# Three moves around the scan and the norms of an RWKV-7 layer: late row splits, steps of 5, block products ten matmuls later

## The chip, the cores and the metric

The kernel runs on one core of a Trainium2 chip. The metric is the device time of one execution in microseconds, as the median of several runs. Besides the runs there is one profiled execution, whose trace gives every instruction of the engines: TensorE (PE, with its weight loads as PEld), VectorE (DVE), ScalarE (ACT), GpSimd (POOL) and SyncE (SP), which issues most DMAs. Each engine goes through its own instructions in the order in which they were put.

## The reference, cut to what matters

Two residual layers on x of 512 tokens by 2048 channels, all in float32: layer 0 is gated differential attention, layer 1 is gated RWKV-7 time mixing with 32 heads of 64 channels. The change lies in layer 1:

```python
p = h @ w_in                                   # r, k, v, g, and two narrow projections
p = p + (token_shift(p) - p) * mu
...
kk = kk / max(norm(kk), 1e-12); k = k * (1 + (a - 1) * k_a)
y = wkv7_scan(r, decay, k, v, -kk, kk * a)     # S = S*w + (S a) b^T + v k^T ; y = S r, token by token
y = (y - mean(y)) * rsqrt(var(y) + GN_EPS) * gn_w + gn_b      # per head: the "norm" below
y = y + sum(r * k * r_k) * v
y = y * silu(g)
x = x + y @ w_out                              # the out-projection
```

## The kernel before, in words

Channels lie on the 128 partitions, tokens along the free axis, so that a tile of 128 x 512 holds one pair of heads for all tokens. Every large product is done as three matmuls of 128x512 on operands split in two parts (`mm3`, L124): hi x hi, hi x lo, lo x hi. Weights come in as `wraw`, ACT casts the hi part `wh` (L105), DVE makes the lo part `wl` (L106). In the same way a row of 128 channels of y that goes into the out-projection is split into `hH` (ACT, L452) and `hL` (DVE, L453), a "row split".

Layer 1 goes through 16 rounds, j = 0 to 15, one for each pair of heads. In a round PE does the projections of pair j (and of the next pair's keys and receptances), and between their matmuls the scan of pair j-1. The scan is in chunks: 512 tokens are 8 chunks, and within a chunk the recurrence is solved as a triangular system.

- `gram` (L1345 pt, L1362 gp) makes the products of a pair inside its chunks out of `AR` (L1335) and `BK`. `t_solve` (L1410 to L1430, 31 short pairs of DVE steps L1421 and L1423) solves a triangular half; its result goes through DRAM (`td`, written in L1431, loaded as `TT` in L1450).
- `t_combine` joins the halves: DVE transposes T out of TT (L1460, two instructions, one per head), PE makes the block products px (L1466), ACT copies X (L1469), PE makes the second block products (L1477) and ACT copies them into TT (L1480).
- `scan_pair` has 8 steps. In each PE makes sm out of the state VS and G (L1559), ACT copies it as rhs (L1562), PE multiplies rhs with TT (L1570), ACT copies VS (L1572), PE makes the product with BKT (L1577), and DVE makes the next VS (L1581, the first time L1584). So every step goes three times from PE to another engine and back. Then come the outputs Y (L1599, L1603) and the subtraction of the mean (L1614 to L1616).
- `group_norm` makes the rest of the norm: squares (ACT, L1625), their sum (L1627), a dozen small steps for the reciprocal root (L1628, L64 to L71) and yc times rsg (L1631). `finish_y` transposes yc on PE (L1638) and adds it into y (L1640). `gated` multiplies with the gate (L1532) and writes the row of y into DRAM (`yd`, POOL, L1533).
- `gate` makes the gate's tile mixv out of its projection: ACT L1188, DVE L1189, ACT's tanh L1521, DVE L1525.

What sets the order of the scan among the projections is the `Chain`: the steps of `chain(...)` are a generator that yields the number of large matmuls to pass before the next step; `tick` counts them. `delay` is the first of these numbers, `lead` stands ahead of the two transpositions L1460, `GAP_T` = 8 ahead of px, `GAP_X` = 10 ahead of L1477, `gap` and `gap_s` are the distances between the products of the scan. `lead` has a default of 10 and an entry of its own in `leads` for some rounds (LAG is 2). A scheduler then orders the instructions of each engine by priority and by what each needs; `issue_after(ins)` makes it place an instruction behind another.

After round 15 the last pair's chain runs among the gate projections of pairs 14 and 15 and the first part of the out-projection. The out-projection takes 16 rows of y: rows 0 to 13 are loaded from `yd` by SP (L462) into eight tiles (the later six rows use the tiles of the first six again) and split; rows 14 and 15 are split from mixv and mixE in place. The gate tile mixv is one buffer: L1188 of pair 14 overwrites the one out of which row 13 is written to DRAM.

## Time and profile before

| | |
|---|---|
| median of the runs | 2062.27 us (2060.34 to 2063.82) |
| the profiled execution's own time | 2061.87 us |
| its span | 2060.2 us |
| PE busy | 2041.7 us, 99% |
| DVE busy | 1608.8 us, 78% |
| ACT busy | 1135.5 us, 55% |
| POOL busy | 385.2 us, 19% |
| TensorE clock granted | 1.0 over the span |

Line numbers are those of the kernel above. In a timeline row stand the start in us from the span's start, the duration in us, the engine, the line, the operation with out<-in, the shapes, how many instructions the row joins, and in brackets the idle time of the engine ahead of it with what ended it. In the chain that ended last a row has start, duration, engine, tile and line. A row of the waits names the waiting instruction, the one waited for, and total, times and longest in us.

### The profile page before, as it was taken

What the parts mean: (1) busy time and instruction counts of PE and PEld (TensorE: products, weight loads), DVE (VectorE), ACT (ScalarE), POOL (GpSimd) and SP (SyncE); (2) the same over time, 40 slices, a digit from 0 to 9 for tenths busy, and PEclk for the clock granted to TensorE, in tenths of its full rate; (3) what the DMA queues carried; (4) which work ended last, traced back from release to release, by engine and by line L of the source; (5) the groups of instructions that cost most, each with busy time, mean ns of one, the idle gap of its engine ahead of it and who ended that gap; (6) DMA issues with size and microseconds to landing.
All of it is one profiled execution on the core that took longest, in us unless ns stands there. A gap on an engine that the chain in (4) does not pass through costs nothing.

```text
span 2060.2 us, 34171 instructions
## 1 busy us (share of the span) xinstructions
PE 2041.7 (99%) x11922; PEld 1675.0 (81%) x11922; DVE 1608.8 (78%) x4104; ACT 1135.5 (55%) x2262; POOL 385.2 (19%) x774
## 2 busy tenths in 40 slices
PE   9999999999999999999999999999999999999999
PEld 7888888888888888888877788888888888877887
DVE  7988988888888977575787888877777888767745
ACT  5765656565666544365565555555555555545423
POOL 1020111102011000101122322322222222231011
PEclk9999999999999999999999999999999999999999
DMA  8487978879787965733323323233333232346676
GB/s 285 157 163 192 178 173 184 164 193 163 190 178 170 267 218 175 171 95 107 103 77 93 92 82 96 87 96 98 98 98 98 86 96 82 111 127 200 212 180 144
DMA packets 159533, 297.76 MB, mean 145 GB/s; under 512 B 64528, under 2 KB 81936, under 8 KB 159360
## 3 DMA queue, kind: packets, MB, share of 16 engines
q1 hardware_dynamic: 110768, 184.39, 28.7%
q0 software_dynamic: 25952, 90.88, 23.3%
q10 hardware_dynamic: 22640, 20.30, 3.1%
q8 instruction: 94, 1.54, 0.3%
q14 instruction: 79, 0.65, 0.1%
HBM read 271.33 MB, written 24.18 MB: 143 GB/s over the span
## 4 chain that ended last, share of the span: by engine, by line
PE 88%; DVE 7%; ACT 3%; issue 1%; DMA 1%; ACTq 0%; SPq 0%; DVEq 0%
PE pp L124 45%; PE pp L575 23%; PE pt L124 5%; DVE wl L106 2%; PE gp L1362 2%; PE sc L124 1%; PE sm L1559 1%; PE o L124 1%; PE sm L1577 1%; PE sm L1570 1%; ACT wh L105 1%; PE Y L1599 1%; PE lora L1104 1%; PE pt L297 1%; PE z L124 1%
## 5 line engine op out<-in xcount | busy, mean ns | idle before, releaser
L106 DVE TENSOR_TENSOR wl<-wraw,wh 128x1024 fp32r<-128x1024 f32 (+1 forms) x286 | 349.9, 1223 | 165.8 <-ACT wh L105 159.1
L105 ACT CAST wh<-wraw 128x1024 fp32r<-128x1024 f32 (+1 forms) x286 | 299.4, 1047 | 237.3 <-PE pp L124 122.1
L124 PE MATMUL pp<-hL,wh 128*128 128x512 f32 x1024 | 413.8, 404 | 0.0
L124 PE MATMUL pp<-hH,wh 128*128 128x512 f32 x1024 | 412.9, 403 | 0.4 <-ACT wh L105 0.4
L124 PE MATMUL pp<-hH,wl 128*128 128x512 f32 x1024 | 413.1, 403 | 0.0
L124 PEld LDWEIGHTS pp<-hH,wh 128*128 128x128 f32 x1024 | 193.1, 189 | 34.8 <-ACT wh L105 0.6
L124 PEld LDWEIGHTS pp<-hL,wh 128*128 128x128 f32 x1024 | 193.1, 189 | 33.5
L124 PEld LDWEIGHTS pp<-hH,wl 128*128 128x128 f32 x1024 | 193.3, 189 | 32.6
L575 PE MATMUL pp<-wh,hH 128*128 128x512 f32 x448 | 176.8, 395 | 0.0
L575 PE MATMUL pp<-wh,hL 128*128 128x512 f32 x448 | 175.7, 392 | 0.0
L124 PE MATMUL pp<-wl,hH 128*128 128x512 f32 x376 | 147.5, 392 | 0.0
L124 PE MATMUL pp<-wh,hH 128*128 128x512 f32 x376 | 147.0, 392 | 0.3 <-ACT hH L1148 0.3
L124 PE MATMUL pp<-wh,hL 128*128 128x512 f32 x376 | 147.2, 392 | 0.1
L1421 DVE SCALAR_TENSOR_TENSOR tmpl<-LT,Tm 128x60 f32<-128x60 f32 (+24 forms) x496 | 135.0, 272 | 13.2
L575 PE MATMUL pp<-wl,hH 128*128 128x512 f32 x448 | 140.3, 392 | 0.0
L1565 POOL COPY SA<-VS 64x64 f32<-64x64 f32 x224 | 55.1, 246 | 398.5 <-DVE VS L1581 376.4
L1423 DVE TENSOR_TENSOR Tm<-Tm,tmpl 128x60 f32<-128x60 f32 (+24 forms) x496 | 103.6, 209 | 11.7
L1562 ACT COPY rhs<-sm 64x64 f32<-64x64 f32 x256 | 52.8, 206 | 85.6 <-PE sm L1559 82.9
L575 PEld LDWEIGHTS pp<-wl,hH 128*128 128x128 f32 x448 | 84.4, 188 | 17.2
L575 PEld LDWEIGHTS pp<-wh,hH 128*128 128x128 f32 x448 | 84.2, 188 | 17.3 <-issue 0.3
L575 PEld LDWEIGHTS pp<-wh,hL 128*128 128x128 f32 x448 | 84.2, 188 | 16.2
L1572 ACT COPY VS<-sm 64x64 f32<-64x64 f32 x256 | 52.7, 206 | 77.2 <-PE sm L1570 71.1
(432 smaller groups left out, 4375.0 us busy)
## 6 DMA issues: line engine op xcount, KB each, us to landing
wraw<-in_rw_w_in_dram SPq DMA_DIRECT2D x128, 512.0 KB
wraw<-in_da_w_in_dram SPq DMA_DIRECT2D x75, 512.0 KB
wraw<-in_da_w_in_dram POOLq DMA_DIRECT2D x28, 512.0 KB, 6.4
wraw<-in_da_w_out_dram SPq DMA_DIRECT2D x26, 512.0 KB
wraw<-in_rw_w_out_dram SPq DMA_DIRECT2D x24, 512.0 KB
Ta<-in_da_w_in_dram POOLq DMA_DIRECT2D x21, 512.0 KB, 5.6
Tb<-in_da_w_in_dram POOLq DMA_DIRECT2D x21, 512.0 KB, 5.8
Tc<-in_da_w_in_dram POOLq DMA_DIRECT2D x21, 512.0 KB, 5.5
```

The lines of the kernel that those rows point to most:

```text
L105: a = nc.scalar.copy(hi[:, ks], raw[:, ks])
L106: d = nc.vector.tensor_sub(lo[:, ks], raw[:, ks], hi[:, ks].bitcast(F32))
L124: m = nc.tensor.matmul(out, a, b, start=s, stop=e, skip_group_check=skip)
L297: nc.tensor.transpose(pt[:, c * P : (c + 1) * P], t1s[t][:, c * P : (c + 1) * P], g.ident[:])
L575: m = nc.tensor.matmul(out[t][:], x, wt[lo][:, k, :], start=first, stop=end and lo == 1 and k == KG - 1, skip_group_check=True)
L1104: m = nc.tensor.matmul(pts[i][:, s], wt[:, c : c + P], x[k][:, s], start=k == 0 and s.start == 0 and c < 2 * P and x is g.hH, stop=k == KT ...
L1362: m = nc.tensor.matmul(gp[h][:, i * P : (i + 1) * P], BK[r_, c0 + i, :, :], p.AR[r_, c0 + i, :, :], start=True, stop=True)
L1421: nc.vector.scalar_tensor_tensor(tt, LT[:, i : i + 1, i + 1 :].to_broadcast([P, s, n]), n2[:, i : i + 1], Tm[:, 0:s, i : i + 1].to_broadca ...
L1423: nc.vector.tensor_add(Tm[:, 0:s, i + 1 :], Tm[:, 0:s, i + 1 :], tt)
L1562: nc.scalar.copy(rhs[r_, :], sm[r_, h * C : h * C + C])
L1565: nc.gpsimd.tensor_copy(p.SA[r_, c - 1, :], VS[r_, c, h, :])
L1572: g.copied = nc.scalar.copy(VS[r_, c, h, :], sm[r_, P : P + C])
```

## The change

It has three parts. `group_norm` returns its last instruction (L1631), and the splits of rows 2 and later are placed behind the one of pair 14's norm. In round 15 the scan of pair 14 has five large matmuls between its products instead of four, and the last pair's chain starts after 10 instead of 24 matmuls. In round 5 (LAG + 3) the lead of pair 4's block products is 16 instead of 10.

```diff
@@ group_norm
-    nc.vector.tensor_mul(yc[:], yc[:], rs[:, :, None].to_broadcast([P, NG, C]))
+    return nc.vector.tensor_mul(yc[:], yc[:], rs[:, :, None].to_broadcast([P, NG, C])).ins
@@ layer1
-                gaps = ((6, 8) if j > LAG + 1 else (5, 6)) if full else (4, 4) if j > LAG else (4, 5)
-                leads = {1: 72, LAG: 18, LAG + 1: 42}
+                gaps = ((6, 8) if j > LAG + 1 else (5, 6)) if full else (5, 5) if j > LAG else (4, 5)
+                leads = {1: 72, LAG: 18, LAG + 1: 42, LAG + 3: 16}
@@
-        chain(g, j, p, 24, 4, 5, lead=34)
+        chain(g, j, p, 10, 4, 5, lead=34)
@@
-        group_norm(g, j - 1, pairs[j - 1])
+        normed = group_norm(g, j - 1, pairs[j - 1])
@@
-        rows = split_rows(g, g.yd2, ("r", "k", "th0", "th1", "l", "f", "xH", "xL"), 1, j - 1)
+        rows = split_rows(g, g.yd2, ("r", "k", "th0", "th1", "l", "f", "xH", "xL"), 1, j - 1, 2, (normed,))
```

On PE in round 5 the first block products px of pair 4 (L1466) move behind the gram of pair 5 (pt and gp); the rows with a minus are before, those with a plus after:

```order
 L124 MATMUL pp<-hL,wh 128x512
 L124 MATMUL pp<-hH,wl 128x512
-L1466 MATMUL px<-T_12733,G_12087 32x32 x16
 L1345 MATMUL pt<-k_12624,ones 32x128 x4
 L1362 MATMUL gp<-AR,BK 128x128 x16
+L1466 MATMUL px<-T_12733,G_12087 32x32 x16
```

The second block products L1477 came directly behind gp and now come ten matmuls behind px; the scan of pair 4 follows ten matmuls later.

On DVE in round 6, behind the subtraction of pair 4's mean (L1616), where T is transposed for pair 5 (L1460), before:

```order
L1616 TENSOR_TENSOR yc<-Y,s_13391 128x4x64 x2
L1460 STREAM_TRANSPOSE T_13420<-TT_9502 64x256 x2
L1627 TENSOR_REDUCE var<-ysq 128x8
L1628 TENSOR_SCALAR var<-var 128x8
L64 TENSOR_SCALAR rs_i<-var 128x8
```

and after:

```order
L1616 TENSOR_TENSOR yc<-Y,s_13401 128x4x64 x2
L1460 STREAM_TRANSPOSE T_13420<-TT_9502 64x256
L106 TENSOR_TENSOR wl<-wraw,wh 128x1024
L1189 SCALAR_TENSOR_TENSOR mixr<-pp,mu,mixr 128x511
L1460 STREAM_TRANSPOSE T_13420<-TT_9502 64x256
L1335 TENSOR_TENSOR AR<-mixr,E 128x8x64
```

The two transpositions stood together; now a weight's lo part and the mix of the receptances (mixr) stand between them.

On DVE at the norm of pair 14, from its sum L1627 on, after:

```order
L1627 TENSOR_REDUCE var<-ysq 128x8
L1189 SCALAR_TENSOR_TENSOR mixv<-pp,mu,mixv 128x511
L1460 STREAM_TRANSPOSE T_20219<-TT_9502 64x256
L1628 TENSOR_SCALAR var<-var 128x8
L453 TENSOR_TENSOR hL<-yr,hH 128x512
L1460 STREAM_TRANSPOSE T_20219<-TT_9502 64x256
L64 TENSOR_SCALAR rs_i<-var 128x8
L1525 SCALAR_TENSOR_TENSOR mixv<-thg,mixv 128x512
L65 TENSOR_SCALAR rs_i<-rs_i 128x8
L453 TENSOR_TENSOR hL<-yr,hH 128x512
L68 TENSOR_TENSOR rs_t<-rs_i 128x8
```

From there to L1631 follow only small steps and one wl. Before, L1189 and the transpositions stood behind four row splits and half of the small steps, and seven row splits stood ahead of L1631. On PE, 66 matmuls, px and 6 matmuls stood between the outputs Y of pair 14 and L1638; now 45 matmuls stand there, and px follows L1638 after 7 more. Ahead of Y stand 23 matmuls more than before, counted from the second step's L1577 of the same scan.

## The prediction

> **What bounds the kernel now.** I read the page's busy times first, then PE's waits, then the timelines of the places that the change touches.

> ```profile
> PE 2041.7 (99%) x11922; PEld 1675.0 (81%) x11922; DVE 1608.8 (78%) x4104; ACT 1135.5 (55%) x2262; POOL 385.2 (19%) x774
> ```

> PE is busy in 2041.7 us, 99% of the span. The change adds and removes no matmul, so it can move the end only through PE's pauses. PE's waits, with total us, times, longest:

> ```profile
> PE sm L1559 <- DVE VS L1581: 3.1, 6, 0.9
> PE pt L1638 <- DVE yc L1631: 1.8, 2, 1.5
> PE px L1466 <- DVE T L1460: 1.0, 1, 1.0
> PE sm L1570 <- ACT rhs L1562: 1.0, 2, 0.8
> ```

> Three lines answer to the three edits: L1559 and L1570 are scan products, L1638 a transposition behind a norm, and L1466 is the block product of pair 4. Together they are 6.9 us, 0.33% of the run: the most that this could bring if nothing were put in place of the waits, except that short pauses around the scan's products don't all appear as waits (below).

> **Part one: leads 16 for the fifth pair (round j=5).** The rows are PE's, then DVE's, then DVE's of round j=6 and PE's of round j=4.

> ```profile
> 1228.39 0.24 PE L1466 MATMUL px<-T,G 32*32 32x32 f32 x2
> 1229.67 0.69 PE L1466 MATMUL px<-T,G 32*32 32x32 f32 x30 [1.04 <-DVE T L1460]
> ...
> 1230.65 2.06 PE L1362 MATMUL gp<-AR,BK 64*128 64x128 f32 x32
> ```

> ```profile
> 1226.94 0.44 DVE L1460 STREAM_TRANSPOSE T<-TT 64x256 f32<-64x256 f32 x1 [1.89 <-DMA TT<-td]
> 1227.31 1.18 DVE L106 TENSOR_TENSOR wl<-wraw,wh 128x1024 fp32r<-128x1024 f32 x1
> ...
> 1229.18 0.44 DVE L1460 STREAM_TRANSPOSE T<-TT 64x256 f32<-64x256 f32 x1
> 1229.65 0.69 DVE L1335 TENSOR_TENSOR AR<-mixr,E 128x512 f32<-128x512 f32 x1
> ```

> ```profile
> 1283.56 0.91 DVE L1460 STREAM_TRANSPOSE T<-TT 64x256 f32<-64x256 f32 x2 [0.53 <-DMA TT<-td]
> ```

> ```profile
> 1174.16 0.69 PE L1477 MATMUL px<-TT,X 32*32 32x32 f32 x32
> ```

> In round 5 px starts at 1228.39, stops after the first half because the second transposition only ends at 1229.62, and ends at 1230.36: 1.97 us for 0.69 of work, 1.28 lost. The change puts pt and gp ahead of px. But gp reads AR, and DVE's order there is unchanged: AR ends at 1230.34, so gp starts at about 1230.40, not at 1230.65. Only 0.25 is won at gp, while px, which used to lie ahead of it and inside that pause, now follows it with its 0.69. L1477 stands by itself ten matmuls later, as in round 4, where its row has the same 0.69: nothing, or at most 0.1 for the pipeline's restart. Net: -0.25 + 0.69 + 0.05 = **+0.5** for round 5, with bounds of -1.3 (if AR came earlier, all of the pause goes) and +0.6.

> All of pair 4's scan moves ten matmuls later with it, so its Y in round 6 stands 22 instead of 32 matmuls ahead of the next px. In round 6 both transpositions were done at 1284.47 in one row and no px waited. With the change DVE's order there becomes exactly that of round 5: one transposition, wl, mixr, the second transposition, AR. I take it that round 5's pause comes back there: up to 1.28, nothing at the least if DVE gets through sooner; I take **+1.0** since order and distance (22 matmuls from Y) equal those of round 5. Part one together: +1.5, from -1.3 to +1.9.

> **Part two: pair 14's scan in steps of 5 instead of 4 (round 15).** PE's rows for the ends, the chain that ended last for one step, DVE's for the wait of a VS:

> ```profile
> 1835.10 0.38 PE L1577 MATMUL sm<-VS,BKT 128*128 128x128 f32 x2
> ...
> 1858.41 1.20 PE L1599 MATMUL Y<-VS,G 128*64 128x64 f32 x32
> ```

> ```profile
> 1843.45 0.49 PE sm L1577 x2
> 1843.93 0.94 PE pp L124 x4
> 1844.90 0.47 PE sm L1559 x2
> 1845.93 0.45 PE sm L1570 x2
> 1846.95 0.49 PE sm L1577 x2
> ```

> ```profile
> 1844.04 0.28 DVE L1581 SCALAR_TENSOR_TENSOR VS<-sm,gam,Sg 64x64 f32<-64x64 f32 x1 [0.57 <-PE sm L1577]
> ```

> From the second step's L1577 to Y are 23.31 us. In them stand 61 matmuls at 0.94/4 = 0.235 (14.3 us), 18 rows of scan products and a transposition row at about 0.25 of PE's pace each (4.75; an estimate, as a row of two lasts 0.49 by itself but the next work starts under its end): 19.1 of work, so 4.2 us are lost, mostly as gaps too short to show as waits. One step shows why: L1577 to L1577 is 1846.95 - 1843.45 = 3.50 us, but its eight matmuls (1.88) and three rows of products (0.75) fill only 2.6 of it; the rest is the way from a product through DVE or ACT and back, which the 4, 2 and 2 matmuls between do not cover. The change puts five between each: 15 x 0.235 + 0.75 = 4.3 us of work against a loop that took 3.50 with its pauses in. So most pauses close. What is left: DVE also has the solve's steps and now and then a wl (1.18 in its row above) in front of a VS, and ACT a weight cast in front of a rhs. I take 0.25 in each of six steps, **1.5**, from 0.4 to 3.0 (nearly all of the 3.1 of L1559 in the table). Gain 4.2 - 1.5 = **-2.7**, from -3.8 to -1.2. The 23 more matmuls that now stand ahead of Y are taken from behind it: Y ends 23 x 0.235 - 2.7 = 2.7 later.

> **Part three: rows 2 and later behind the norm; delay 24 to 10.** Rows of PE, DVE, POOL and ACT; SP's load of row 8, whose cast is ACT's second row; and the landings of the row tile:

> ```profile
> 1859.54 0.68 PE L1603 MATMUL Y<-SA,AR 64*64 64x64 f32 x28
> ...
> 1879.20 0.63 PE L1638 MATMUL pt<-ident,yc 128*128 128x128 f32 x4 [1.54 <-DVE yc L1631]
> ```

> ```profile
> 1866.45 0.69 DVE L1532 TENSOR_TENSOR mixv<-mixv,y 128x512 f32<-128x512 f32 x1
> 1867.06 0.17 DVE L64 TENSOR_SCALAR rs_i<-var 128x8 int32<-128x8 int32 x1
> ...
> 1873.21 0.75 DVE L1189 SCALAR_TENSOR_TENSOR mixv<-pp,mu,mixv 128x511 f32<-128x511 f32 x1
> ...
> 1878.37 0.68 DVE L1631 TENSOR_TENSOR yc<-yc,rsg 128x512 f32<-128x512 f32 x1
> ```

> ```profile
> 1867.45 0.57 POOL L1533 DMA_DIRECT2D yd<-mixv  x1 [0.60 <-DVE rs_i L65]
> ```

> ```profile
> 1872.49 0.69 ACT L1188 ACTIVATE mixv<-pp,omu 128x512 f32<-128x512 f32 x1 [2.04 <-DMA yd<-mixv]
> ...
> 1876.38 0.62 ACT L452 CAST hH<-yr 128x512 fp32r<-128x512 f32 x1 [0.20 <-DMA yr<-yd]
> ```

> ```profile
> 1872.19 0.85 SPq L462 DMA_DIRECT2D yr<-yd  x2
> ```

> ```profile
> DMA to landing us min/median/max: 2.4/4.6/6.5
> ```

> Before, L1631 ended 18.8 us after Y's last product (1860.22 to 1879.05), with seven row splits (L453, of L1532's shape and 0.69) among its small steps; PE had 72 matmuls and px to do meanwhile and still waited 1.54. Now only two splits stand ahead of L1631, but L1638 also stands only 45 matmuls behind Y: 45 x 0.235 = 10.6 us. And DVE's new order has L1189 of pair 14's gate ahead of both splits and of the norm's small steps. L1189 waits for ACT's L1188, which overwrites mixv and so waits for the row DMA from the same tile: from L1532's end (1867.14) to L1188 were 5.35 us. In the new order L1532 comes ahead of Y's L1614, so I put its end at Y - 0.75 (an estimate). L1188 then starts at Y + 4.6 and, 0.69 later, L1189 at Y + 5.3. From there DVE has L1189 (0.75), two halves of a transposition (0.44 each), L1525, two splits and L1631 (four of 0.69, some 0.1 of each overlapped), wl (1.18) and some dozen small steps (0.17, 0.2 with the gap between): 7.7 in all, Y + 13.0. PE is there at Y + 10.6 and waits 2.4, where it waited 1.54, or 1.6 with its restart: **+0.8**. With a landing 2.6 sooner, in the 2.4 of the last row, this wait would go and what is late next (T's load, row 1's split) leave some 0.5 of one: -1.1; with 6.5 it would be +2.3. Behind the waiting L1188 ACT has the casts of rows 1 to 3, and none but row 1's is needed ahead of L1638.

> [...]

> At the last pair's own norm the second of the two L1638 waits, 1.8 - 1.5 = 0.3, goes: wl leaves the middle of its small steps. **-0.3**, at the least 0. The last pair's scan keeps its gaps of 4 and 5: nothing.

> **The sum.** +1.5 - 2.7 + 0.8 - 0.3 = -0.7 on the profiled run's 2061.87 us gives 2061.2; the median of the runs shown, 2062.27, lies 0.4 above that run, so **2061.6** by the median.

> **The rivals.**
> *All pauses go and none comes back*: AR is early in round 5 (-1.3), px finds T ready in round 6 (0), the scan gives -3.8, L1638's two waits go (-1.6 and -0.3). That is -7.0, 2055.3. For it: each pause is short, and little would close it. Against it: AR in round 5 and the DMA behind L1188 are late for reasons that the change leaves. It is faster by over 0.2% once four of the seven come. Chance 0.11.
> *The row DMA lands early* (in 2.4 us): the norm's term is -1.1 instead of +0.8, 2059.7. Against it stands the 5.04 from issue to L1188 of the same instruction in the row above. Chance 0.13.
> *The late rows delay the last scan*: slower. Rows 8 to 13 use the tiles of rows 0 to 5 and load only when those are split, which now is partly behind the norm. In ACT's new order row 12's cast stands ahead of the last pair's first rhs (L1562). Row 12's load can leave only after row 4's split, about 1.5 behind L1638; row 8's load took 1876.38 - 1872.19 = 4.19 to its cast. So the cast would end 6.3 behind L1638, where rhs, after 25 matmuls, two px and a product on PE (5.9 + 1.4 + 0.25), is wanted 7.5 behind it. Past 5.4 us for the load each us is a us of PE. On SP rows 10 to 12 now stand behind three residual rows and a weight load that were behind them before, or beside them; their landing may take 11, which costs 5.6 and gives 2067.2. From 10.2 on it is slower by over 0.2%. Against it: no row load of before kept a cast waiting for more than the 0.20 in its row. Chance 0.11.
> *The forecast*, a mix of gains and returned pauses: 0.65.

> **How the numbers follow.** The forecast's bounds, if all fell to one side: -1.3 - 3.8 - 1.1 - 0.3 = -6.5 and 1.9 - 1.2 + 2.3 = +3.0. They hardly all do: downwards I go to about two thirds of it, 2058.0, which takes in the early landing and leaves out the first rival; upwards to 2065.8, past the bound and most of the way to the slow rival. Under 0.2% (4.1 us) a change can hardly be told from none here. Faster by more is the first rival and a little of the forecast's edge, 0.13; slower by more is the third, 0.11; 0.76 lie between.

> **What the new profile would show.** Right: in round 5 gp starts at about 1230.4 behind AR, no px wait there, and one of about 1 us at pair 5's px in round 6; PE's waits for L1559 at 1.5 or less in place of 3.1; Y of pair 14 ending near 1862.9; L1638 waiting 2 to 3 us, with L1189 behind "DMA yd" as the reason. Wrong: a scan whose steps still stretch by a wait on VS or rhs; L1638 without a wait; a wait of several us at the last pair's first L1559 or L1570, with L452 ahead of L1562; or a difference outside of the three places.

## The result: slower by 0.36%, and the profile after

The changed kernel takes 2068.04 us (median of seven runs, 2066.88 to 2073.85) against 2062.23 us (2060.34 to 2063.82): a ratio of 1.0036, 95% interval 1.0026 to 1.0045. Its profiled execution has a span of 2065.6 us, 5.4 more than before, and took 2067.32 us. PE's waits after:

```profile
PE pt L1638 <- DVE yc L1631: 6.4, 2, 6.2
PE sm L1559 <- DVE VS L1581: 3.2, 8, 0.8
...
PE gp L1362 <- DVE AR L1335: 1.3, 1, 1.3
PE px L1466 <- DVE T L1460: 0.9, 1, 0.9
PE sm L1570 <- ACT rhs L1562: 0.8, 1, 0.8
```

One wait is new in size: L1638 behind the norm of pair 14, 6.2 us where it was 1.5. The two waits that the lead was forecast to leave, gp in round 5 and px in round 6, are there. The timelines at the norm, PE first:

```profile
1863.47 0.68 PE L1603 MATMUL Y<-SA,AR 64*64 64x64 f32 x28
...
1880.75 1.09 PE L1638 MATMUL pt<-ident,yc 128*128 128x128 f32 x4 [6.16 <-DVE yc L1631]
1881.49 0.78 PE L124 MATMUL pp<-hH,wh 128*128 128x512 f32 x1
1882.06 0.63 PE L124 MATMUL pp<-hL,wh 128*128 128x512 f32 x1
1882.49 0.63 PE L124 MATMUL pp<-hH,wl 128*128 128x512 f32 x1
```

Then DVE's:

```profile
1867.17 0.68 DVE L1627 TENSOR_REDUCE var<-ysq 128x8 f32<-128x512 f32 x1
1871.34 0.75 DVE L1189 SCALAR_TENSOR_TENSOR mixv<-pp,mu,mixv 128x511 f32<-128x511 f32 x1 [3.49 <-ACT mixv L1188]
1874.13 0.44 DVE L1460 STREAM_TRANSPOSE T<-TT 64x256 f32<-64x256 f32 x1 [2.04 <-DMA TT<-td]
1874.49 0.12 DVE L1628 TENSOR_SCALAR var<-var 128x8 f32<-128x8 f32 x1
...
1879.91 0.69 DVE L1631 TENSOR_TENSOR yc<-yc,rsg 128x512 f32<-128x512 f32 x1
```

Between the norm's sum and its next small step DVE stood still twice, 3.49 us for L1188 and 2.04 us for pair 15's TT load, although neither has to do with the norm: they only stand ahead of it in DVE's queue. From the first L1460 on, the rest took 6.5 us, where the prediction's sum had some 7. ACT's row, then SP's and POOL's, for what was awaited:

```profile
1870.62 0.69 ACT L1188 ACTIVATE mixv<-pp,omu 128x512 f32<-128x512 f32 x1 [3.67 <-DMA yd<-mixv]
```

```profile
1862.49 0.38 SPq L1431 DMA_DIRECT2D td<-Tm  x1
1868.33 1.81 SPq L1450 DMA_DIRECT2D TT<-td  x4
```

```profile
1862.99 0.78 POOL L680 DMA_DIRECT2D frow<-yd  x1 [3.11 <-DVE Tm L1430]
1864.06 0.57 POOL L1533 DMA_DIRECT2D yd<-mixv  x1 [0.28 <-DVE mixv L1532]
1864.62 1.43 POOL L680 DMA_DIRECT2D frow<-yd  x2
```

The td store took 5.84 us until the TT loads could leave (3.81 before), those took 5.80 more until L1460 (2.92 before), and the write of row 13 (yd, the row write below) took 6.56 us from its issue to L1188 (5.04 before). Three loads of 512 KB each (frow, L680, for the out-projection's sums; L680 stands in `sum_forms`) leave between 1862.99 and 1866.05, around the store and the row write. Before, two of them left at 1860.22, ahead of the store.

And the clock fell. The columns of these stretches are the bounds and length in us, the busy time and count of PE, PEld, DVE, ACT and POOL, then TensorE's granted clock (1.00 is full speed, 0.50 the "half clock" below), the DMA share and GB/s:

```profile
1874.00:1880.00 6.00, 0.59 (x3) 0.17 (x1) 5.54 (x19) 3.08 (x6) 0.00 (x0) 0.80 0.57 170
1880.00:1882.00 2.00, 1.25 (x5) 1.25 (x6) 1.93 (x4) 0.55 (x1) 0.00 (x0) 0.50 0.88 245
1882.00:1884.00 2.00, 2.00 (x6) 1.55 (x5) 1.82 (x3) 0.00 (x0) 0.00 (x0) 0.50 1.02 341
1884.00:1886.00 2.00, 2.00 (x37) 1.34 (x37) 0.91 (x1) 1.66 (x3) 0.57 (x1) 0.89 0.98 264
```

During the pause the granted clock went to 0.50 and stayed there until about 1884.4: 6.8 us in all, of which PE worked some 3.6. The matmuls behind L1638 come every 0.43 us instead of 0.23: some 1.8 us more.

Comparing the time at which the n-th large matmul starts in both traces gives the account: -1.1 us by round 4 (no cause in the change), +1.9 in rounds 5 to 8 (the lead), -2.4 over pair 14's scan, +6.8 from L1638 to the last pair's norm, and nothing later. Of the 6.8, 4.6 are the longer wait of L1638 and some 1.8 the half clock; the other 0.4 were not traced to a cause.

### The profile page after: what moved, and what is told of

It is laid out like the page before. It is cut to its first block, busy times and chain, and to the rows that moved or that the text cites. A ratio compares the mean times of both kernels' runs of the same rounds, so it can differ in the third digit from the quotient of the medians.

```text
span 2065.6 us, 34164 instructions
## 1 busy us (share of the span) xinstructions
PE 2042.7 (99%) x11922; PEld 1677.7 (81%) x11922; DVE 1612.6 (78%) x4104; ACT 1134.2 (55%) x2262; POOL 387.2 (19%) x774
## 3 DMA queue, kind: packets, MB, share of 16 engines
q8 instruction: 94, 1.54, 0.3%
## 4 chain that ended last, share of the span: by engine, by line
PE 86%; DVE 9%; ACT 2%; DMA 1%; issue 1%; ACTq 0%; SPq 0%; POOL 0%; DVEq 0%; POOLq 0%
PE pp L124 44%; PE pp L575 22%; PE pt L124 5%; DVE wl L106 2%; PE gp L1362 2%; PE sc L124 1%; PE sm L1559 1%; PE o L124 1%; PE sm L1577 1%; PE sm L1570 1%; DVE tmpl L1421 1%; PE Y L1599 1%; DVE Tm L1423 1%; PE lora L1104 1%; ACT wh L105 1%
## 5 line engine op out<-in xcount | busy, mean ns | idle before, releaser
L106 DVE TENSOR_TENSOR wl<-wraw,wh 128x1024 fp32r<-128x1024 f32 (+1 forms) x286 | 351.0, 1227 | 166.6 <-ACT wh L105 159.8
L124 PE MATMUL pp<-hH,wh 128*128 128x512 f32 x1024 | 413.9, 404 | 0.4 <-ACT wh L105 0.4
L124 PE MATMUL pp<-hL,wh 128*128 128x512 f32 x1024 | 414.0, 404 | 0.0
L124 PE MATMUL pp<-hH,wl 128*128 128x512 f32 x1024 | 413.8, 404 | 0.0
L124 PEld LDWEIGHTS pp<-hH,wh 128*128 128x128 f32 x1024 | 193.5, 189 | 34.8 <-ACT wh L105 0.6
L124 PEld LDWEIGHTS pp<-hL,wh 128*128 128x128 f32 x1024 | 193.5, 189 | 33.6
L124 PEld LDWEIGHTS pp<-hH,wl 128*128 128x128 f32 x1024 | 193.6, 189 | 33.0
L124 PE MATMUL pp<-wl,hH 128*128 128x512 f32 x376 | 148.0, 394 | 0.0
L124 PE MATMUL pp<-wh,hH 128*128 128x512 f32 x376 | 147.6, 393 | 0.0
L124 PE MATMUL pp<-wh,hL 128*128 128x512 f32 x376 | 147.0, 391 | 0.0
L1562 ACT COPY rhs<-sm 64x64 f32<-64x64 f32 x256 | 52.8, 206 | 94.7 <-PE sm L1559 91.8
```

Of the source, the lines that this page charges most:

```text
L106: d = nc.vector.tensor_sub(lo[:, ks], raw[:, ks], hi[:, ks].bitcast(F32))
L124: m = nc.tensor.matmul(out, a, b, start=s, stop=e, skip_group_check=skip)
L1562: nc.scalar.copy(rhs[r_, :], sm[r_, h * C : h * C + C])
```

## The experiments

In all of them "before" ran beside on the same chip; ratios are to it, with 95% intervals. f1, f2, f3, g2 and g3 ran once each, in the profiler, so each of their numbers is that of one execution; beside f1 to f3 before took 2060.15 us (2058.95 to 2061.05), beside g2 and g3 2061.62 (2059.97 to 2063.67). The theory after the result: the lead costs 1.9, the scan of 5 brings 2.4, and the 6.8 come from DVE's queue, in which two DMA waits now stand ahead of the norm, with the half clock on top (A). The rival: the late row splits make it slow (B).

**The parts alone.**

e1, the lead alone:

```diff
-                leads = {1: 72, LAG: 18, LAG + 1: 42}
+                leads = {1: 72, LAG: 18, LAG + 1: 42, LAG + 3: 16}
```

> Only the lead of 16 for pair 4 is changed. Theory A (from the two traces): the px pause moves, it does not go; gp waits about 1.5 us for AR in round 5 and px about 1 us for T in round 6, in all +1.9 us against the kernel before (between rounds 4 and 8), nothing elsewhere. Rival: the round-6 pause has to do with the other two parts or with chance; then the time is the same or 1 us less.

Measured: 1.0010 (1.0001 to 1.0020), and in the trace +1.95 us between rounds 4 and 6. PE's waits are those of the changed kernel:

```profile
PE gp L1362 <- DVE AR L1335: 1.4, 1, 1.4
PE px L1466 <- DVE T L1460: 0.8, 1, 0.8
```

The pause was doubled, not moved away.

e2, the steps of 5 alone:

```diff
-                gaps = ... (4, 4) if j > LAG else (4, 5)
+                gaps = ... (5, 5) if j > LAG else (4, 5)
```

> Only the steps of 5 in pair 14's scan. The scan's pauses fall by about 2.6 us as in the changed kernel. Theory A: with Y later, VectorE's queue gets the gate's L1189 and the transpositions L1460 ahead of the norm's small steps, and both wait for DMAs; L1638 stands 72 matmuls behind Y, L1631 at about Y + 26 with twelve row splits in between, so L1638 waits about 8 us, and the clock drops to half for some us: in all about +4 to +6 us. Rival B (late rows are what makes it slow): -2.6 us.

Measured: 1.0016 (1.0007 to 1.0025), span 2063.9. The scan's gain is there (2.4 us up to Y), and behind it the same picture without any late row split: the first L1460 waited 2.65 us for its load and L1638 and a weight's lo part took the delay.

```profile
PE pt L1638 <- DVE yc L1631: 2.3, 1, 2.3
PE pp L124 <- DVE wl L106: 2.3, 1, 2.3
```

The sign was as theory A had it. L1638's own wait was 2.3 and not 8: a part came out at the wl, and each of the two pauses was followed by 3.4 us of half clock.

e3, the late row splits alone:

```diff
-    nc.vector.tensor_mul(yc[:], ...)
+    return nc.vector.tensor_mul(yc[:], ...).ins
...
-        group_norm(g, j - 1, pairs[j - 1])
+        normed = group_norm(g, j - 1, pairs[j - 1])
...
-        rows = split_rows(..., 1, j - 1)
+        rows = split_rows(..., 1, j - 1, 2, (normed,))
```

> Only the late row splits. The scan stays as before, L1189 and L1460 come behind L1631 on VectorE. Theory A: L1631 ends at about Y + 12 and L1638, 50 matmuls behind Y, waits 0.3 us or less instead of 1.54; with the last norm's 0.3 that is -1.5 us. Rival B (late rows are what makes it slow): a wait of several us at L1638 or at the last pair's scan, +3 us or more.

Measured: 1.0007 (0.9997 to 1.0016). Neither B nor the gain of A: the first L1460 slipped in ahead of L1631 and waited there for its load, so L1638 waited 1.74.

```profile
1871.25 0.44 DVE L1460 STREAM_TRANSPOSE T<-TT 64x256 f32<-64x256 f32 x1 [1.11 <-DMA TT<-td]
1871.62 0.64 DVE L1631 TENSOR_TENSOR yc<-yc,rsg 128x512 f32<-128x512 f32 x1
```

e4, the changed kernel with the row splits as before:

```diff
-        rows = split_rows(..., 1, j - 1, 2, (normed,))
+        rows = split_rows(..., 1, j - 1)
```

> The changed kernel with the row splits as before: steps of 5, delay 10 and the lead stay. Theory A: as with the steps of 5 alone a long wait at L1638, or at the last scan's first products, 6 us or more, and the half clock; with the lead's +1.9 in all +5 to +8 us. Rival B: faster than before by about 1 us.

Measured: 1.0019 (1.0009 to 1.0029), span 2063.0, so 2.6 under the changed kernel, and not 6 us of wait; L1638 stands further back there and waits for nothing, but L1477 waits 1.96 us for ACT's X, behind row casts that wait for their loads. B falls as the main cause: without late splits it is still slower. But beside the other parts they do cost something, these 2.6 us, which alone (e3) they did not show.

g4, the changed kernel with the old lead:

```diff
-                leads = {1: 72, LAG: 18, LAG + 1: 42, LAG + 3: 16}
+                leads = {1: 72, LAG: 18, LAG + 1: 42}
```

> The changed kernel with the lead of round 5 as before. By the traces the lead costs 1.9 us between rounds 4 and 8 and nothing later, so the span falls from 2065.6 to about 2063.7; the 6 us wait at L1638 and the 6.8 us of half clock stay. Rival: the lead's cost is made up later, and the span stays at 2065.6.

Measured: 1.0022 (1.0013 to 1.0031), span 2064.2, L1638's wait 6.0. The half clock lasted 3.4 us here, not 6.8. Taken out here the lead is worth 1.4 us of the span, put in alone (e1) it cost 1.9.

**What holds DVE, and why it is late.**

f1, a tile of its own for pair 14's gate:

```diff
-        gts = [gate(g, j - 1, gps)]
+        gts = [gate(g, j - 1, gps, "g0")]
```

> The changed kernel, with pair 14's gate in a tile of its own, so that L1188 does not overwrite the tile out of which row 13 is written. Theory P (the prediction's step: the row DMA ahead of L1188 holds VectorE): L1189 starts some 4 us sooner, and the 6.16 us wait of L1638 falls by about 3 us, the half clock goes. Rival Q (T's load is what ends last): L1189 comes early, but the first L1460 still stands ahead of the norm's steps and waits till about 1874; L1638's wait stays at 6 to 7 us.

Measured: span 2066.4, 2068.06 us.

```profile
1867.03 0.74 DVE L1189 SCALAR_TENSOR_TENSOR mixg<-pp,mu,mixg 128x511 f32<-128x511 f32 x1
1874.22 0.44 DVE L1460 STREAM_TRANSPOSE T<-TT 64x256 f32<-64x256 f32 x1 [6.45 <-DMA TT<-td]
```

```profile
1881.56 1.08 PE L1638 MATMUL pt<-ident,yc 128*128 128x128 f32 x4 [6.91 <-DVE yc L1631]
```

L1189 came 4.3 us sooner and nothing was won: Q holds, P falls. The prediction had named the earlier of two waits; the one behind it ended last.

f2, the three frow loads held back, by a copy of one column of rsg into each tile ahead of its load, so that the load has to wait for the norm (the fourth load in that stretch, the first to leave, stays):

```diff
+                if i == 1 or i == 0 and r is rows[0]:
+                    nc.vector.tensor_copy(r[:, 0, 0:1], g.normed_rs)
                 nc.gpsimd.dma_start(out=r, in_=src[...])
...
+    if j == 14:
+        g.normed_rs = rs[:, 0:1]
```

> The changed kernel, with three 512 KB loads of POOL (frow) held back until pair 14's norm by a one-column copy into each tile. Theory R (these loads slow the td store, the TT loads and the row write that run beside them): T's first L1460 starts at about 1870 instead of 1874.1, L1189 at about 1869.5 instead of 1871.3, L1638's wait falls to about 3 us, the half clock goes or is short, span 2061 to 2062. Rival S (the loads have nothing to do with it): L1460 stays at 1874.

Measured: span 2059.9 against 2065.6, clock 1.0; 2061.56 us. Line numbers are higher by 2 to 4 in the runs with held loads, as the added lines shift them. SP, ACT, DVE and PE:

```profile
1862.02 0.38 SPq L1433 DMA_DIRECT2D td<-Tm  x1
1866.06 1.81 SPq L1452 DMA_DIRECT2D TT<-td  x4
```

```profile
1867.09 0.69 ACT L1190 ACTIVATE mixv<-pp,omu 128x512 f32<-128x512 f32 x1 [1.17 <-DMA yd<-mixv]
```

```profile
1868.48 0.43 DVE L1462 STREAM_TRANSPOSE T<-TT 64x256 f32<-64x256 f32 x1
```

```profile
1875.82 0.63 PE L1642 MATMUL pt<-ident,yc 128*128 128x128 f32 x4 [1.52 <-DVE yc L1635]
```

The td store fell from 5.84 to 4.04 us, the row write from 6.56 to 3.52 (POOL issued it at 1863.57), L1462 found its data there, and the wait is 1.52. Counted by the n-th large matmul, 1.3 us are lost behind Y instead of 6.8: this one edit takes back 5.5 of them. It is not quite back at before, which took 2060.15 us beside it; the 1.4 left are no more than the lead costs. R holds, S falls.

The other runs agree. In the six in which all three loads leave around the td store (the changed kernel, e2, e4, f1, f4, g4), the store took 5.4 to 6.0 us; in the seven with held loads (f2, f3, g1 to g3, h1, h2) 3.4 to 4.2. Through what the loads slow the store was not tried.

f3, both of these edits, f1's and f2's:

> The changed kernel with both: the gate in its own tile and the three frow loads held. With R and Q the wait of L1638 is set by T's load alone, about 2 to 3 us; with P and S it falls by 3 us as with the tile alone; with P and R it is about 1 us.

Measured: span 2059.9, L1642 waits 0.4 at the most, as R with P. Once the loads are out of the way, the tile does bring 1.1 us at that place, which it could not bring alone; the span is no less, as this execution was 0.6 later already ahead of that place.

g3, f2's edit in the kernel before, as a control:

> The kernel before, with the three frow loads held: what the hold does by itself. There the loads leave at 1860 and 1866, around the td store and the row write. L1638's wait of 1.54 us falls by at most 1 us; span 2059 to 2060.5. If it falls by 3 us or more, the hold is a gain of its own and says less on the change.

Measured: span 2059.9 against 2060.2. The L1642 wait fell by 1.2, to 0.3, a little more than said, and 0.7 of it came back at the last pair's first products. So there the hold is worth 0.5 us of waits, not 5, and in time nothing that shows (2061.63 against 2061.62 us beside it).

f4, gate and transpositions placed behind the norm, delay 24:

```diff
-        chain(g, j, p, 10, 4, 5, lead=34)
+        chain(g, j, p, 24, 4, 5, lead=34)
...
-        gts = [gate(g, j - 1, gps)]
+        g.centred = normed
+        with tc.issue_after(normed):
+            gts = [gate(g, j - 1, gps)]
```

> The changed kernel, with pair 14's gate and pair 15's transpositions L1460 placed behind the norm's last step L1631, and the delay of the last chain back at 24. If what stands in VectorE's queue is the cause, L1631 ends at about Y + 8.5, L1638 (33 matmuls behind Y) waits 1 us or less, the clock stays at 1.0, and the span is about 2058.5: 6 to 7 us under the changed kernel, 1 to 2 us under the one before. If the scan of 5 or the late splits cost by another way, it stays above 2062.

Measured: 1.0028 (1.0017 to 1.0039), span 2066.0: a miss, and above the 2062 that was to tell of another cost. The trace shows two. L1188 still waits for the row write on ACT, and the cast of row 1 stands behind it there; DVE's lo part of row 1, ahead of L1631, waited 2.49 us for it. So the row write reached the norm by way of ACT's queue, and L1638 waited 2.8. And in round 5 of this execution gp's pause was 1.87 us, and the clock fell to half there too (0.50 for 6.8 us), which cost 3 us at a place that the edit doesn't touch.

**A version that is faster?**

g1, the changed kernel with f1's and f2's edits and g4's (the old lead):

> The changed kernel without the lead of 16, with the three frow loads held behind pair 14's norm and pair 14's gate in a tile of its own. If the parts add up as read from the traces (scan -2.5, norm wait down from 1.5 to about 0.5, no half clock, no pause in round 6), the profiled span is about 2057.5 to 2058.5 and the time 0.1% under the kernel before. If the lead's +1.9 isn't its own, the span stays at 2059.9.

Measured: span 2058.3, 0.9993 (0.9984 to 1.0002).

g2, and the same timed as h1: of the change only the steps of 5 (e2's edit), with f2's hold:

> The steps of 5 alone, with the three frow loads held behind the norm; row splits as before. If the loads are what made the steps of 5 alone 3.7 us slower in the profile (waits of 2.3 us each at L1638 and at a weight's lo part, both followed by half clock), the first L1460 comes 5 us sooner, those waits fall under 1 us, the clock stays full, and the span is about 2058. Rival (the many row splits ahead of L1631 do it): L1638 still waits 2 us or more and the span stays at 2062 or above.

Measured: span 2057.6, 2059.33 us, clock 1.0.

> The steps of 5 with the three frow loads held, row splits and lead as before, now timed. If the steps of 5 are the one part of the change that is worth keeping once the DMAs are out of the way, the profiled span is again near 2057.6 and the median 0.1% under the kernel before. If the late rows were needed, it lies above the version with all parts but the lead (2058.3).

Measured: 1.0003 (0.9994 to 1.0012), eleven runs from 2057.83 to 2064.84, span 2063.1, clock 0.998. One program, two executions on two chips, 5.5 us apart; the eleven runs on one chip spread by 7.0. Of the 5.5, 1.9 came in round 5, where a px pause of 1.27 us was followed by half clock (1.15 and none in the first execution), and most of the rest at L1642. L1642 in the first and in the second, the row behind it with it:

```profile
1882.39 0.63 PE L1642 MATMUL pt<-ident,yc 128*128 128x128 f32 x4 [1.74 <-DVE yc L1635]
```

```profile
1885.23 0.73 PE L1642 MATMUL pt<-ident,yc 128*128 128x128 f32 x4 [2.81 <-DVE yc L1635]
...
1887.90 0.63 PE L124 MATMUL pp<-wh,hL 128*128 128x512 f32 x1
```

The longer pause was followed by 3.4 us of half clock, the shorter one by none.

h2, with f1's tile as well:

> The same with pair 14's gate in a tile of its own. If the row write ahead of L1188 still holds VectorE by 1.7 us as in the profile without the tile, L1189 starts sooner, L1638's wait of 1.9 us falls by 1 us or more, and the span is about 2056.5. If the row splits ahead of L1631 are what is last now, it stays at 2057.6.

Measured: 0.9991 (0.9983 to 1.0000), span 2059.8, eleven runs from 2057.59 to 2061.50. L1191 came at 1865.46 instead of 1867.05, but L1642 still waited 1.6: DVE was busy nearly throughout with row splits, two wl and the gates' steps between the norm's small steps, so the row splits, by far the most of these, are the likely last; no run took them away there. g1 and h2 are the best of those timed, 0.07% and 0.09% under the kernel before, with intervals that reach 1. Whether the late splits bring anything of their own stays open: g1, with them, and h2, without, can't be told apart.

## Why the prediction was wrong, step by step

**The lead: right.** Forecast +1.5, measured +1.9 between the traces of before and after and in e1, by the mechanism told: gp behind AR (its start at 1229.03, a us earlier than told, as all of that trace is by then) and px waiting for T in round 6, 0.86 us, with the order of round 5.

**The scan: right in the cost, wrong in one sign.** Forecast -2.7, measured -2.4 in the changed kernel, and the same in e2. Over the prediction's own stretch, from the second step's L1577 to Y:

```profile
1836.46 0.38 PE L1577 MATMUL sm<-VS,BKT 128*128 128x128 f32 x2
...
1862.34 1.20 PE L1599 MATMUL Y<-VS,G 128*64 128x64 f32 x32
```

That is 25.88 us against 23.31, for 23 more matmuls of 0.235 (5.4): 2.8 less. Y ended at 1864.15 instead of 1862.9: 1.1 of that lay ahead of the scan. The sign "L1559 at 1.5 or less in place of 3.1" did not come, it stayed at 3.2, and could not have: of the 3.1 only 0.40 lay in this scan, and of L1570's 1.0 only 0.19; the rest stands in earlier rounds, from 1036 to 1202, which the change leaves. So the 6.9 us of "three lines" were not the pauses that this change could take away. What closed were the gaps too short to show as waits, as the prediction had worked out.

**The norm: this step failed.** Forecast +0.8, with bounds of -1.1 and +2.3; measured +6.8 with what follows it. The place and the order were right, and that L1189 would stand in the way. PE came to L1638 at Y + 10.4, as forecast (10.6), but L1631 ended at Y + 16.5 instead of Y + 13.0: 1.9 later by L1188 (Y + 6.5 instead of 4.6), 2.0 by T's load, 0.5 sooner by the steps behind it. Three things were wrong in the step. First, T's load was not in the sum: L1460 stood in the quoted order, but its load's landing was not worked out, and it ended last (f1). The prediction names it as what would be late next were the row write early; that it could be later than the row write it does not weigh, though DVE had waited for this load in the kernel before too:

```profile
1872.62 0.44 DVE L1460 STREAM_TRANSPOSE T<-TT 64x256 f32<-64x256 f32 x1 [1.10 <-DMA TT<-td]
```

Second, the DMA times of before were carried over unchanged (5.35 from L1532 to L1188), although the change moves Y, the end of the solve and so the start of three 512 KB loads onto the same moment; f2 shows that without these loads 6.16 - 1.52 = 4.6 us of the wait are gone. POOL's other loads, which wait for Y and L1430, were not looked at as what a later Y moves. Third, the pause was priced as its own length, without the half clock, some 1.8 us here; in e2 pauses of 2.27 and 2.31 us, about the forecast's 2.4, were each followed by half clock too.

From its issue to L1190 the row write took 2.90 (g3), 3.52 (f2) and 4.09 us (g2) with the loads held; to L1188, with them beside it, 5.14 (e4) to 6.56 (the changed kernel). Before, it was 5.04.

**The last norm's 0.3** did not come either: its L1638 still waits 0.27. **The slow rival** (row 12's cast ahead of the last scan's rhs) did not happen: the first rhs found its row casts done. Casts waited for row loads (1.56 and 1.36 us on ACT), but during L1638's pause, where they cost nothing. So the sign came out as that rival had it, by another mechanism, and that its 2067.2 lies near the 2068.0 measured is chance.

## What to carry to other kernels

Before an instruction is moved on an engine, list every DMA that is awaited ahead of it there in the new order (here DVE stood still for 3.49 and 2.04 us ahead of the norm's next small step), and what else leaves at that moment (here the same write took 3.52 us with the three loads held and 6.56 with them beside it); a step that ends later moves all loads that wait for it. When a wait is taken away that stands in front of another, ask what the second ends at; here the first was worth nothing until the second was gone. Price a pause of TensorE with what the traces show of the clock afterwards: here all nine of 1.87 us or more were followed by 3.4 or 6.8 us at 0.50, and of the shorter ones some were (1.27 and 1.60 us) and some were not (ten of 1.42 to 1.74 us).

## What the runs showed of the hardware

In these profiles, after pauses of PE of 1.87 (f4), 1.96 (e4), 2.27 and 2.31 (e2), twice 2.81 (f4, h1), 6.0 (g4), 6.16 (the changed kernel) and 6.91 us (f1) the granted clock was 0.50, for 3.4 us, or for 6.8 in three cases (those of 6.16, of 6.91 and of 1.87); after pauses of 1.42 to 1.74, ten in all, it stayed at 1.0; and in h1 and h2 it fell also after 1.27 in round 5 and 1.60 at L1642. So among the pauses of 1.27 to 1.74 us either was seen, among those of 1.87 us or more the half clock each time.
